# One decoder layer on one core: attention values summed by query tile, split, mean and exponential moved, first and last stage rearranged

## The chip, the core and the metric

The kernel runs on one core of a Trainium2 chip. TensorE (PE) multiplies, VectorE (DVE), ScalarE (ACT) and GpSimd (POOL) work on tiles in SBUF, SyncE (SP) issues most DMAs. The metric is the device time of one execution in microseconds (us); smaller is better. The inputs lie in HBM, and the output goes back there.

## The reference

One layer over 256 tokens of width 2048, in float32. A normed input is projected; 16 query heads in 4 groups attend in three branches (compressed blocks, selected blocks, window), a convolution module works beside them, both go through one output projection, and a gated feed-forward block follows.

```python
h = rms_norm(x, mix_norm_g[l])
proj = h @ w_in[l]
q, kv, gate_logits, conv_in = jnp.split(proj, splits, axis=-1)
...
attn = nsa_attention(q, kv, gates, rel_bias, cmp_pos[l], cmp_w1[l], cmp_w2[l])
conv = conformer_conv(conv_in, conv_w[l], conv_b[l], conv_ln_g[l], conv_ln_b[l])
x = x + jnp.concatenate([attn, conv], axis=-1) @ w_out[l]
h = rms_norm(x, ffn_norm_g[l])
x = x + conv_glu_ffn(h, w_up[l], ffn_conv_w[l], ffn_conv_b[l], w_down[l])
```

At 256 tokens there are only four selectable blocks, so "selected" and "window" both are causal attention over all keys, each with its own keys and values; each query tile therefore has, per head, two softmaxes of 256 queries by up to 256 keys, and one over 15 compressed keys. The convolution module gates, convolves 31 taps per channel, subtracts the mean over channels, divides by the deviation and applies a swish.

## The kernel before

**Numbers in two halves.** Each float32 operand is split into a high part in the fast matmul format (made by ACT, a cast) and a low part (the rest, by DVE or POOL, a subtraction). A product is three matmuls: high by high, high by low, low by high (`mm3`, L142 to L144; `mm_rows`, L149 to L151). Weights come in chunks of 1 MB, one DMA each on SP's queue (L91), three buffers deep, and are split two chunks ahead (`w_split`: ACT L110; DVE or, for chunks 5 to 31, POOL at L115).

**Stages.** (1) A head: the first two weight chunks (chunk 0 and 1, the gate and value halves of convolution channels 0 to 127) come packed with the transposed input in six pieces (`CUTS`: four pieces of 2 of the 16 blocks of the inner dimension, then two pieces of 4); each piece is split by ACT (L234, L239) and DVE (L235, L240) and multiplied at once into banks 0 and 1. (2) The other convolution inputs, keys and values, with the convolution's taps on DVE beside them. (3) Eight query chunks (`tile_chunk`), each 128 columns, and the attention of their heads. (4) The output projection, the feed-forward up and down products. (5) The last rows: sums of squares, a power on POOL (L174), scaling on ACT (L1019) and DVE (L1020), output DMAs (L1022).

**What sets the order around the change.** The order is written by hand: each engine executes in the order of the program. A chunk of 48 matmuls has four hooks, one after each 12. A hook may run an attention tick (`attn_tick`), the steps that queue behind (`behind`, `conf`, `steps`), and one piece of a weight split. `late` holds what is done when the next chunk begins, such as taking a finished query tile out of its bank (`q_out`: DVE L638).

**Attention.** A query tile i has four units n = 4i .. 4i+3: two head halves r times two branches br. A tick with number n does the values of unit n-7 (`st_out`, L770, L774), the transposes of unit n-5 (L754), the scores of a pair of units when n is even (`st_scores`, L712, L713; bank 2 and bank 4 or 5), the reciprocal of sums (`st_rec`, L741, L742), the bias and minimum (`st_min`, DVE L722, reads the scores), the copy of transposes (`st_evac`, ACT L759), the scaling (`st_scale`, POOL L748) and the exponential (`st_exp`, ACT L733). The values of both r are summed when the second r of a branch is there: once for br 0, and once for br 1, the latter followed by the compressed values (L774) and the split of the result (L776, L777).

**Beside it.** The compressed branch of a tile pair m runs in steps: scores (L657), logits and exponential (`cmp_exp`, L663 to L672), probabilities (L677 to L680), transposes (L685). The convolution's mean (`conf_mean`, L430, and its copy L426), the subtraction from y (`conf_apply`, DVE L444, 128x512), squares (ACT L449) and their sums (DVE L452) are steps of `conf`, started by `conf_center` when query chunk 1 begins. The query's split (`q_split`) makes a high part on ACT (L644) and a low part on DVE (L645), at a hook.

```python
for f, d in ((st_out, DEEP), (st_transpose, D_T), (st_scores, 0), (st_rec, D_S), (st_min, 1),
             (st_evac, D_T), (st_scale, D_S), (st_exp, 1)):
```

Of the kernel before, what the change touches and what calls it, by code (L numbers as in the profile page):

```python
# [17 lines left out]
P = 128  # L18
# [21 lines left out]

def head_of_slot(s):
    i, r = divmod(s, 2)
    return (i // 4) * 8 + r * 4 + i % 4
# [3 lines left out]
def hybrid_trunk(ctx: ExitStack, tc: tile.TileContext, a: dict, out: bass.AP):  # L47
# [31 lines left out]
    st = {"dma": 2, "split": 2, "use": 0}  # L79
# [110 lines left out]
    with ExitStack() as mx:  # L190
# [27 lines left out]
        for _ in range(3):  # L218
            w_dma()
# [11 lines left out]
        for (lo, hi), (xc, *wc) in zip(CUTS, heads):  # L231
            for k in range(lo, hi):
                xk = xc[:, (k - lo) * T:(k - lo + 1) * T]
                nc.scalar.activation(xt_h[:, k], xk, AF.Copy, scale=mix_g[:, k:k + 1])  # L234
                nc.vector.scalar_tensor_tensor(xt_l[:, k], xk, mix_g[:, k:k + 1], xt_h[:, k].bitcast(F32),  # L235
                                               op0=OP.mult, op1=OP.subtract)
            sl = slice(lo * P, hi * P)
            for (h, l), raw in zip((parts[0], parts[1]), wc):
                nc.scalar.activation(h[:, sl], raw, AF.Copy)  # L239
                nc.vector.tensor_sub(l[:, sl], raw, h[:, sl].bitcast(F32))  # L240
# [107 lines left out]
        ysum = wk.tile([P, T], F32, name="ysum", bufs=1)  # L348
        summed = []

        def conf_add(j):
            summed.append(j)
            if len(summed) > 1:
                nc.vector.tensor_add(ysum, y[:, summed[0]] if len(summed) == 2 else ysum, y[:, j])
# [37 lines left out]
        for j in range(8):  # L392
            gb, ab = [b[:, :T] for b in bank[2 * (j if j < 3 else (j + 1) % 2):][:2]]
            if j == 0:
                pair = [w_next(2), w_next(2, 1)]
                for lo, hi in CUTS:
                    for ps, (wh, wl) in zip((gb, ab), pair):
                        for k in range(lo, hi):
                            sl = slice(k * P, (k + 1) * P)
                            mm3(ps, wh[:, sl], wl[:, sl], xt_h[:, k], xt_l[:, k], k == 0, k == KD - 1)  # L400
                w_pump()
                first = gb, ab
                continue
            tile_chunk(gb)
# [17 lines left out]
        cf = {}  # L422

# [56 lines left out]
        def conf_center():  # L480
            conf.extend((
                no, no, conf_mean, no, lambda: conf_apply(OP.subtract, 0), lambda: conf_apply(OP.subtract, 2),
                lambda: conf_sq(0, 0), lambda: (conf_sq(2, 2), conf_apply(OP.subtract, 4)),
                lambda: conf_apply(OP.subtract, 6), lambda: conf_fold(2, 2),
                lambda: conf_sq(4, 2), no, lambda: conf_fold(2, 2), lambda: conf_sq(6, 2), no,
                lambda: conf_fold(2, 2), no, lambda: conf_fold(1, 1)))
# [153 lines left out]

        def q_split(i):
            for r in range(2):
                h, o = slice(64 * r, 64 * r + 64), slice(64 - 64 * r, 128 - 64 * r)
                nc.scalar.activation(qs[h, i % 4, r], q32[i][h], AF.Copy)  # L644
# [4 lines left out]
        pct = ap.tile([P, 4, T], F32, name="pct", tag="oh")  # L649
        pcb = ap.tile([P, 2, 4, 32], F32, name="pcb")  # L650
        nc.gpsimd.memset(pcb[:, :, :, NCMP:], 0.0)

# [8 lines left out]
        def cmp_exp(m):  # L661
            cm["e"] = e = wk.tile([P, 2, 4, NCMP], F32, name="ec", bufs=1)
            nc.gpsimd.memset(e[:, 0, :, NC0:], BIG)  # L663
# [5 lines left out]
            mn = wk.tile([P, 2, 4], F32, name="mnc", bufs=1)  # L669
            nc.vector.tensor_reduce(mn, e, axis=mybir.AxisListType.X, op=OP.min)  # L670
            nc.vector.tensor_sub(e, e, mn[:, :, :, None].to_broadcast([P, 2, 4, NCMP]))
            nc.scalar.activation(e, e, AF.Exp, scale=-1.0)  # L672
# [9 lines left out]
        def cmp_tr(m):  # L682
# [4 lines left out]
            nc.scalar.activation(pct[:, m], pg[:, :T], AF.Copy)  # L687
# [69 lines left out]
        def st_evac(n):  # L757
            es = wk.tile([P, 384], F32, name="es", bufs=5)
# [3 lines left out]
        def st_out(n):  # L762
            i, r, br = units[n]
            if r == 0:
                return
            es, o, q = [US.pop(n - 2), US.pop(n)], bank[7], i // 4
            kw = dict(skip_group_check=True)
            for b, cols in enumerate((slice(0, T), slice(P, T))):
                for rr in range(2):
                    nc.tensor.matmul(o[64 * rr:64 * rr + 64, cols], vt[:, b, br, q, rr],  # L770
                                     es[rr][:, :T] if b == 0 else es[rr][:, T:], start=br + b == 0, stop=False, **kw)
            if br == 1:
                assert cbst["done"] > i // 2
                nc.tensor.matmul(o[:, :T], vc[:, i % 2, i // 4].rearrange("p r n -> p (r n)"), pct[:, i // 2],  # L774
                                 start=False, stop=True, **kw)
                nc.scalar.activation(ma_h[:, i], bank[7][:, :T], AF.Copy)  # L776
# [359 lines left out]
```

## Time and profile before

| what | us |
| --- | --- |
| median of 3 runs | 1116.58 |
| lowest, highest | 1116.53, 1116.62 |
| profiled execution, its own time | 1115.1 |
| its span, first to last instruction | 1113.3 |
| PE busy in the span | 1098.0 |
| DVE, ACT, POOL busy | 770.4, 577.6, 188.1 |

The page counts an engine as busy while an instruction runs on it; times within the span are measured from its start. A wait is idle time of an engine before an instruction, put down to what came last. Matmul ends are modelled, so idle time of PE between two matmuls reads a little short; distances from start to start are exact. The granted TensorE clock is 0.998 over the span.

### The profile page before, as it was taken

Reading aid. Unit: us, or ns where it says so; the run is one execution under the profiler, and the core shown is the slowest. Engines: PE = TensorE matmul, PEld = TensorE weight load, DVE = VectorE, ACT = ScalarE, POOL = GpSimd, SP = SyncE. Lnnn points to the kernel's source line nnn. Section 1 sums busy time; section 2 is a strip of 40 time slices with the busy share of each in tenths; the row PEclk is TensorE's granted clock in tenths of the full one; section 3 lists DMA queues with packets and bytes.
Section 4 is the critical chain, followed back from the end, with each engine's and each line's share of the span. In section 5 each row is a group of like instructions: output and inputs, shape, how many; then the busy total and the mean of one; then the engine's idle time right before and its main releaser. Section 6 shows DMA issues by size and latency. Waiting matters only on the chain.

```text
span 1113.3 us, 16297 instructions
## 1 busy us (share of the span) xinstructions
PE 1098.0 (99%) x6506; PEld 956.6 (86%) x6506; DVE 770.4 (69%) x1262; ACT 577.6 (52%) x836; POOL 188.1 (17%) x143
## 2 busy tenths in 40 slices
PE   9999999899999999999999999999999999999997
PEld 8999999887788888888888888888888888888885
DVE  6799976766456677777777777777778655556554
ACT  7544456777465555554555455545555444444442
POOL 0888765665200000000000000000000000000000
PEclk9999999999999999999999999999999999999999
DMA  9685537222644655555555555555555555555542
GB/s 373 221 295 199 172 98 258 77 81 97 233 171 173 232 190 192 189 190 190 189 189 189 190 189 189 189 190 189 189 189 190 189 188 189 189 189 187 188 155 76
DMA packets 32425, 207.46 MB, mean 186 GB/s; under 512 B 3883, under 2 KB 6203, under 8 KB 8284
## 3 DMA queue, kind: packets, MB, share of 16 engines
q1 hardware_dynamic: 28972, 199.85, 50.4%
q10 hardware_dynamic: 3376, 6.55, 1.6%
q8 instruction: 51, 0.84, 0.3%
q14 instruction: 26, 0.21, 0.0%
HBM read 204.27 MB, written 2.12 MB: 185 GB/s over the span
## 4 chain that ended last, share of the span: by engine, by line
PE 93%; DVE 2%; ACT 1%; POOL 1%; DMA 1%; issue 1%; SPq 0%; POOLq 0%; DVEq 0%; ACTq 0%
PE bank L972 29%; PE bank L990 21%; PE bank L974 14%; PE bank L142 5%; PE bank L144 5%; PE bank L143 5%; PE bank L149 3%; PE bank L150 3%; PE bank L151 3%; PE bank L770 1%; POOL e L748 1%; DMA hb<-in_head 1%; PE bank L754 1%; ACT e L733 0%; PE bank L518 0%
## 5 line engine op out<-in xcount | busy, mean ns | idle before, releaser
L110 ACT ACTIVATE wh<-wraw 128x2048 fp32r<-128x2048 f32 (+2 forms) x239 | 355.7, 1505 | 361.5 <-issue 150.7
L115 DVE TENSOR_TENSOR wl<-wraw,wh 128x2048 fp32r<-128x2048 f32 (+1 forms) x185 | 364.9, 1977 | 195.4 <-ACT wh L110 195.3
L972 PE MATMUL bank<-xt,wh 128*128 128x512 f32 x1408 | 488.7, 394 | 0.0
L974 PE MATMUL bank<-xt,wl 128*128 128x256 f32 x1408 | 390.1, 277 | 0.0
L972 PEld LDWEIGHTS bank<-xt,wh 128*128 128x128 f32 x1408 | 264.0, 188 | 61.2
L974 PEld LDWEIGHTS bank<-xt,wl 128*128 128x128 f32 x1408 | 264.4, 188 | 0.0
L142 PE MATMUL bank<-xt,wh 128*128 128x256 f32 x512 | 146.7, 287 | 1.4 <-ACT wh L239 1.4
L144 PE MATMUL bank<-xt,wl 128*128 128x256 f32 x512 | 145.0, 283 | 0.3 <-DVE wl L240 0.2
L143 PE MATMUL bank<-xt,wh 128*128 128x256 f32 x512 | 144.8, 283 | 0.0
L174 POOL TENSOR_TENSOR rstd<-ms,half 128x1 f32<-128x1 f32 x4 | 2.2, 548 | 809.2 <-DVE ms L167 809.2
L115 POOL TENSOR_TENSOR wl<-wraw,wh 128x1024 fp32r<-128x1024 f32 (+1 forms) x54 | 121.4, 2275 | 28.0 <-ACT wh L110 26.9
L990 PE MATMUL bank<-wh,gh 128*128 128x512 f32 x336 | 105.5, 395 | 0.0
L990 PE MATMUL bank<-wl,gh 128*128 128x512 f32 x336 | 105.5, 395 | 0.0
L990 PE MATMUL bank<-wh,gl 128*128 128x512 f32 x336 | 105.5, 395 | 0.0
L142 PEld LDWEIGHTS bank<-xt,wh 128*128 128x128 f32 x512 | 98.0, 191 | 3.2 <-ACT wh L239 1.9
L144 PEld LDWEIGHTS bank<-xt,wl 128*128 128x128 f32 x512 | 98.0, 191 | 0.7 <-DVE wl L240 0.7
L143 PEld LDWEIGHTS bank<-xt,wh 128*128 128x128 f32 x512 | 98.0, 191 | 0.4
L369 DVE SCALAR_TENSOR_TENSOR bank<-us,cw,bank 128x256 f32<-128x256 f32 x232 | 94.9, 482 | 2.8 <-ACT bank L364 2.1
L935 DVE SCALAR_TENSOR_TENSOR yt<-u,fcw,yt 128x255 f32<-128x255 f32 (+1 forms) x176 | 80.9, 481 | 3.1
L990 PEld LDWEIGHTS bank<-wl,gh 128*128 128x128 f32 x336 | 63.0, 187 | 15.5
L990 PEld LDWEIGHTS bank<-wh,gl 128*128 128x128 f32 x336 | 63.0, 187 | 15.4
L990 PEld LDWEIGHTS bank<-wh,gh 128*128 128x128 f32 x336 | 62.9, 187 | 15.4
(188 smaller groups left out, 1073.8 us busy)
## 6 DMA issues: line engine op xcount, KB each, us to landing
wraw<-in_w_u SPq DMA_DIRECT2D x88, 1024.0 KB, 4.8
wraw<-in_w_d SPq DMA_DIRECT2D x44, 1024.0 KB, 4.8
wraw<-in_w_t SPq DMA_DIRECT2D x30, 1024.0 KB, 5.0
wraw<-in_w_o SPq DMA_DIRECT2D x16, 1024.0 KB, 4.8
wraw<-in_w_vg SPq DMA_DIRECT2D x4, 608.0 KB, 3.7
hb<-in_head SPq DMA_DIRECT2D x2, 1024.0 KB, 9.7
xr<-in_x SPq DMA_DIRECT2D x2, 1024.0 KB, 19.8
wb<-rel_scratch ACTq DMA_DIRECT2D x1, 2048.0 KB, 14.3
```

What stands on the lines that cost most here:

```text
L110: nc.scalar.activation(h[:, sl], raw[:, sl], AF.Copy)
L115: (nc.gpsimd if pooled else nc.vector).tensor_sub(l[:, sl], raw[:, sl], h[:, sl].bitcast(F32))
L142: nc.tensor.matmul(ps, wh, xh, start=first, stop=False)
L143: nc.tensor.matmul(ps, wh, xl, start=False, stop=False)
L144: nc.tensor.matmul(ps, wl, xh, start=False, stop=last)
L149: nc.tensor.matmul(ps, xh, wh, start=first, stop=False)
L150: nc.tensor.matmul(ps, xh, wl, start=False, stop=False)
L369: nc.vector.scalar_tensor_tensor(y[:, j] if last else acc[0], us[:, j, k:k + T], cw[:, j, k:k + 1], acc[0], op0=OP.mult, op1=OP.add)
L935: nc.vector.scalar_tensor_tensor(ys[i][:, d:], us_[i][:, :T - d], fcw[:, c, k:k + 1], ys[i][:, d:], op0=OP.mult, op1=OP.add)
L972: nc.tensor.matmul(bk[i], wh[:, k, sl], xt[:, kt].rearrange("p a t -> p (a t)"), start=kt == 0, stop=False)
L974: nc.tensor.matmul(bk[i][:, :T], wl[:, k, sl], xt_h[:, kt], start=False, stop=kt == KD - 1)
L990: nc.tensor.matmul(banks[n], g[p][:, kt % 4, sl], ws[w][:, k * 1024 + n * 512:k * 1024 + (n + 1) * 512], start=kt + i == 0, stop=i == 2 an ...
```

## The change

The numbers of operations hardly change; places do.

- **Head.** The weights of the third chunk (chunk 2, the gate half of channels 128 to 255) are loaded in two halves, the first between pieces 4 and 5 of the head, the second after piece 6, and multiplied in the head (`next_mm`: blocks 0 to 7 after piece 4, blocks 8 to 15 after piece 6). The first piece's weights are cast by DVE, and its matmuls run all high products of both banks first (`first_mm`).
- **Convolution's mean** starts when query chunk 0 begins, in bank 1; subtractions and squares are packed closer. Its sum and the compressed probabilities share one buffer.
- **Exponential's table** is loaded by a two-element exponential behind the gates.
- **Query split:** the high part follows at once on taking the tile out (`q_high`).
- **Compressed logits** go to a tile of their own, whose masked part is filled once; probabilities come one step sooner for the first three pairs.
- **Attention tick:** the minimum stands ahead of the reciprocal; the values of all four units of a tile run as one group, with one more buffer for the copies.
- **Last rows:** the last sum of squares runs on DVE with the mean in it; the result leaves in pieces of 256, 256 and 512 columns, the very last on ACT's queue.

```diff
+HEAD_NEXT = (0, 0, 0, 8, 8, 16)
...
+            if n == 3:
+                raw2 = wpool.tile([P, CW], F32, name="wraw", bufs=NR)
+            if n in (3, 5):
+                sl = slice((n - 3) * 512, (n - 1) * 512)
+                nc.sync.dma_start(raw2[:, sl], a["w_t"][0][:, sl])
-        for _ in range(3):
+        for _ in range(2):
             w_dma()
...
+            if part == 1:
+                nc.vector.tensor_sub(l[:, sl], raw, h[:, sl].bitcast(F32))
+            elif n == 0:
+                nc.vector.tensor_copy(h[:, sl], raw)
+            else:
                 nc.scalar.activation(h[:, sl], raw, AF.Copy)
...
+                for n, hi in enumerate(HEAD_NEXT):
+                    head_mm((gb, ab), n) if n else first_mm((gb, ab))
+                    w = parts[2] if n < len(CUTS) - 1 else w_next(2, 2)
+                    w_pump()
+                    next_mm(g1, w, at, hi)
+                    at = hi
...
-            cf["b"] = bank[0][:, :T]
-            nc.tensor.matmul(cf["b"], ones, ysum, start=True, stop=True)
+            cf["b"] = bank[1][:, :T]
+            nc.tensor.matmul(cf["b"], ones, cf["sum"], start=True, stop=True)
...
+            ready = wk.tile([P, 2], F32, name="rv", bufs=1)
+            nc.scalar.activation(ready, ones[:, :2], AF.Exp)
...
+        def q_high(i):
+            for r in range(2):
+                h = slice(64 * r, 64 * r + 64)
+                nc.scalar.activation(qs[h, i % 4, r], q32[i][h], AF.Copy)
...
-                nc.scalar.activation(qs[h, i % 4, r], q32[i][h], AF.Copy)
...
+        ecr = ap.tile([P, 2, 4, NCMP], F32, name="ecr")
+        nc.gpsimd.memset(ecr, BIG)
...
-            nc.gpsimd.memset(e[:, 0, :, NC0:], BIG)
...
-                       ((lambda m: None, cmp_scores, cmp_exp, lambda m: None, cmp_probs, lambda m: None, cmp_tr) if m < 3 else
+                       ((lambda m: None, cmp_scores, cmp_exp, cmp_probs, lambda m: None, cmp_tr) if m < 3 else
...
-            i, r, br = units[n]
-            if r == 0:
+            i = n // 4
+            if n % 4 < 3:
                 return
...
+            for br in range(2):
+                es = [US.pop(4 * i + 2 * r + br) for r in range(2)]
...
-            for f, d in ((st_out, DEEP), (st_transpose, D_T), (st_scores, 0), (st_rec, D_S), (st_min, 1),
+            for f, d in ((st_out, DEEP), (st_transpose, D_T), (st_scores, 0), (st_min, 1), (st_rec, D_S),
...
             q_evac(i, bank[i % 2])
+            q_high(i)
             behind.append(lambda: q_split(i))
...
-            if i == 1:
+            if i == 0:
                 fill(1e9)
                 conf_center()
...
+                    nc.vector.tensor_tensor_reduce(out=sqd3, in0=xq, in1=xq, scale=1.0 / D, scalar=acc, op0=OP.mult,
+                                                   op1=OP.add, accum_out=ss3[:, t, 4:5])
...
+            for lo, hi in ((0, 256), (256, 512), (512, 1024)):
...
+                (nc.scalar if lo == 512 and t else nc.sync).dma_start(
```

Three places as the built programs have them. First, DVE where the reciprocal, the compressed probabilities (smc, pcb) and the convolution's subtraction (y) stand between the third query tile's split (qs) and the minimum of unit 6 (e, mn from bank 66, which is bank 2, first half), before the change:

```order
L645 TENSOR_TENSOR qs<-q_2519,qs 64x256 x2
L444 TENSOR_TENSOR y<-y,ck 128x512
L677 TENSOR_REDUCE smc<-ec 128x8
L678 RECIPROCAL smc<-smc 128x8
L679 TENSOR_TENSOR smc<-smc,gates 128x8
L680 TENSOR_TENSOR pcb<-ec,smc 128x8x15
L741 RECIPROCAL lsum<-lsum 128x4
L742 TENSOR_TENSOR lsum<-lsum,gates 128x4
L722 ISA e,mn<-bank_66,wb 128x128
```

And DVE at the same place after it (the lines are those of the changed program: L702 takes the tile out, L713 is the split, L794 the minimum, L813 and L814 the reciprocal):

```order
L747 TENSOR_REDUCE smc<-ec 128x8
L748 RECIPROCAL smc<-smc 128x8
L749 TENSOR_TENSOR smc<-smc,gates 128x8
L750 TENSOR_TENSOR pcb<-ec,smc 128x8x15
L702 SCALAR_TENSOR_TENSOR q_2532<-bank_64,rB 128x256
L794 ISA e,mn<-bank_66,wb 128x128
L794 ISA mn 128x1
L794 ISA e,mn<-bank_68,wb 128x256
L794 ISA mn 128x1
L713 TENSOR_TENSOR qs<-q_2532,qs 64x256 x2
L794 ISA e,mn<-bank_66,wb 128x128
```

The subtraction is gone from there, the probabilities stand ahead of the tile that is taken out, and between the split and the minimum of unit 6 nothing stands. Second, PE where the values of query tile 0 are summed into bank 71 (bank 7), before: the first of its two groups (br 0), and what followed it; the second group (br 1) came after 12 matmuls in all:

```order
L770 MATMUL bank_71<-es,vt 64x256 x2
L770 MATMUL bank_71<-es,vt 64x128 x2
L754 MATMUL bank_67<-ident,e 128x128 x3
L142 MATMUL bank_65<-xt,wh 128x256
L143 MATMUL bank_65<-xt,wh 128x256
L144 MATMUL bank_65<-xt,wl 128x256
```

PE at the values of the same tile after the change:

```order
L147 MATMUL bank_64<-xt,wl 128x256
L845 MATMUL bank_71<-es,vt 64x256 x2
L845 MATMUL bank_71<-es,vt 64x128 x2
L845 MATMUL bank_71<-es,vt 64x256 x2
L845 MATMUL bank_71<-es,vt 64x128 x2
L847 MATMUL bank_71<-pct,vc 128x256
L826 MATMUL bank_70<-ident,e 128x128 x3
```

Both branches now stand side by side, at the tick where the second one stood. Third, ACT from the last gates to the first split query tile, before the change:

```order
L624 ACTIVATE gates<-bank_67,rc 128x16 x3
L110 ACTIVATE wh<-wraw 128x1024 x2
L644 ACTIVATE qs<-q_2314 64x256 x2
L110 ACTIVATE wh<-wraw 128x1024 x2
L426 ACTIVATE ck<-bank_64 128x256
L733 ACT_TABLE_LOAD
L733 ACTIVATE e,lsum<-e,mn 128x128
```

And ACT from the same gates after it:

```order
L686 ACTIVATE gates<-bank_67,rc 128x16 x3
L689 ACT_TABLE_LOAD
L689 ACTIVATE rv<-ones 128x2
L113 ACTIVATE wh<-wraw 128x1024 x2
L488 ACTIVATE ck<-bank_65 128x256
L511 ACTIVATE s_2315<-y 128x512
L708 ACTIVATE qs<-q_2325 64x256 x2
```

The table's load, the mean's copy (ck) and the first squares now stand ahead of the first split query tile.

More of the change, by code (lines that the diff above doesn't have):

```diff
@@ L78, in hybrid_trunk @@
     NR, NB, LA = 3, 3, 2
-    st = {"dma": 2, "split": 2, "use": 0}
+    st = {"dma": 3, "split": 3, "use": 0}
     raws, parts, pieces = {}, {}, []
@@ L230, in hybrid_trunk, with head_x @@
             parts[c] = (wpool.tile([P, CW], F32R, name="wh", bufs=NB), wpool.tile([P, CW], F32R, name="wl", bufs=NB))
-        for (lo, hi), (xc, *wc) in zip(CUTS, heads):
-            for k in range(lo, hi):
-                xk = xc[:, (k - lo) * T:(k - lo + 1) * T]
+        def head_x(n, k, part):
+            lo = CUTS[n][0]
+            xk = heads[n][0][:, (k - lo) * T:(k - lo + 1) * T]
+            if part == 0:
                 nc.scalar.activation(xt_h[:, k], xk, AF.Copy, scale=mix_g[:, k:k + 1])
+            else:
@@ new lines, in head_split, with head_mm @@
+        def head_split(n):
+            ks = range(*CUTS[n])
+            if n == 0:
+                for c in range(2):
+                    head_w(n, c, 0)
+            for k in ks:
+                head_x(n, k, 0)
+                head_x(n, k, 1)
+            for c in range(2):
+                if n:
+                    head_w(n, c, 0)
+                head_w(n, c, 1)
+        def head_mm(pss, n):
+            for ps, (wh, wl) in zip(pss, (parts[0], parts[1])):
+                for k in range(*CUTS[n]):
+                    sl = slice(k * P, (k + 1) * P)
+                    mm3(ps, wh[:, sl], wl[:, sl], xt_h[:, k], xt_l[:, k], k == 0, k == KD - 1)
@@ new lines, in first_mm, with next_mm @@
+        def first_mm(pss):
+            for part in range(3):
+                for k in range(*CUTS[0]):
+                    sl = slice(k * P, (k + 1) * P)
+                    for ps, w in zip(pss, (parts[0], parts[1])):
+                        nc.tensor.matmul(ps, w[part == 2][:, sl], (xt_h, xt_l)[part == 1][:, k],
+                                         start=k + part == 0, stop=False)
+        def next_mm(ps, w, lo, hi):
+            wh, wl = w
+            for k in range(lo, hi):
+                sl = slice(k * P, (k + 1) * P)
+                mm3(ps, wh[:, sl], wl[:, sl], xt_h[:, k], xt_l[:, k], k == 0, k == KD - 1)
@@ L394, in hybrid_trunk @@
             if j == 0:
[L395 to L401, printed above, removed]
+                g1 = bank[2][:, :T]
+                parts[2] = h2, l2 = [wpool.tile([P, CW], F32R, name=nm, bufs=NB) for nm in ("wh", "wl")]
+                for n in range(len(CUTS)):
+                    head_split(n)
+                    if n in (3, 5):
+                        sl = slice((n - 3) * 512, (n - 1) * 512)
+                        nc.scalar.activation(h2[:, sl], raw2[:, sl], AF.Copy)
+                        nc.vector.tensor_sub(l2[:, sl], raw2[:, sl], h2[:, sl].bitcast(F32))
+                w_dma()
+                st["use"] = 2
+                at = 0
+                for n, hi in enumerate(HEAD_NEXT):
[4 more added lines that the diff above has]
+                    at = hi
+                parts.pop(0), parts.pop(1)
                 first = gb, ab
                 continue
-            tile_chunk(gb)
+            if j > 1:
+                tile_chunk(gb)
             if j == 1:
@@ L686, in cmp_tr @@
                                  is_transpose=True, start=True, stop=True)
-            nc.scalar.activation(pct[:, m], pg[:, :T], AF.Copy)
+            if m == 0:
+                cm["t"] = ap.tile([P, 4, T], F32, name="pct", tag="oh")
+            nc.scalar.activation(cm["t"][:, m], pg[:, :T], AF.Copy)
             cbst["done"] = m + 1
@@ L762, in st_out @@
         def st_out(n):
-            i, r, br = units[n]
-            if r == 0:
+            i = n // 4
+            if n % 4 < 3:
                 return
-            es, o, q = [US.pop(n - 2), US.pop(n)], bank[7], i // 4
+            o, q, m = bank[7], i // 4, i // 2
+            assert cbst["done"] > m
             kw = dict(skip_group_check=True)
[L768 to L776, printed above, removed]
-                nc.vector.tensor_sub(ma_l[:, i], bank[7][:, :T], ma_h[:, i].bitcast(F32))
+            for br in range(2):
+                es = [US.pop(4 * i + 2 * r + br) for r in range(2)]
+                for b, cols in enumerate((slice(0, T), slice(P, T))):
+                    for r in range(2):
+                        nc.tensor.matmul(o[64 * r:64 * r + 64, cols], vt[:, b, br, q, r],
+                                         es[r][:, :T] if b == 0 else es[r][:, T:], start=br + b == 0, stop=False, **kw)
+            nc.tensor.matmul(o[:, :T], vc[:, i % 2, q].rearrange("p r n -> p (r n)"), cm["t"][:, m],
+                             start=False, stop=True, **kw)
+            nc.scalar.activation(ma_h[:, i], o[:, :T], AF.Copy)
+            nc.vector.tensor_sub(ma_l[:, i], o[:, :T], ma_h[:, i].bitcast(F32))
         tick = {"n": 0}
```

59 lines of the change are left out of this document (32 added, 27 removed).

## The prediction

> **What bounds the kernel now.** I read the page's busy times first, then the busy times by stage, then what PE waited for, then the timeline around those waits.
>
> ```profile
> PE 1098.0 (99%) x6506; PEld 956.6 (86%) x6506; DVE 770.4 (69%) x1262; ACT 577.6 (52%) x836; POOL 188.1 (17%) x143
> ...
> 0.00:20.00 20.00, 17.28 (x118) 16.37 (x119) 14.15 (x32) 15.59 (x33) 0.69 (x6) 1.00 0.92 361
> 200.00:280.00 80.00, 75.88 (x561) 64.20 (x561) 54.78 (x215) 61.15 (x182) 51.40 (x59) 1.00 0.26 93
> 1104.00:1114.00 10.00, 1.08 (x10) 0.88 (x8) 2.81 (x9) 2.73 (x8) 0.55 (x1) 0.71 0.53 197
> ```
>
> PE is busy for 1098.0 of 1113.3 us, so only three stages can give anything: the head, where it idles 2.7 of 20 us, the attention, where it idles 4.1 of 80, and the end, where 8.9 of 10 pass without it. Outside them only less work or a cheaper order on PE helps. Clock is full (1.00) wherever PE works.
>
> ```profile
> PE bank L712 <- DVE mn L722: 3.7, 4, 2.1
> PE bank L142 <- ACT wh L239: 1.4, 2, 1.1
> ```
>
> PE's waits have names: scores wait for DVE's minimum (four times, the longest 2.1 us), and the head waits for a cast. After the attention PE never idles long again, and its later work doesn't depend on when it starts (weights are there: 0.2 us idle from 280 to 1104), so what is won before 280 reaches the end whole.
>
> **The attention's waits.** This is DVE ahead of the two longest, in rows of its timeline, and PE at the longest:
>
> ```profile
> 199.99 0.28 DVE L670 TENSOR_REDUCE mnc<-ec 128x8 f32<-128x120 f32 x1 [1.20 <-POOL ec L663]
> 200.79 0.28 DVE L722 CUSTOM_DVE_ANT_0 e<-bank,wb 128x128 f32<-128x128 f32 x1
> ...
> 205.07 0.86 DVE L645 TENSOR_TENSOR qs<-q,qs 64x256 fp32r<-64x256 f32 x2 [1.02 <-ACT qs L644]
> 205.94 0.69 DVE L444 TENSOR_TENSOR y<-y,ck 128x512 f32<-128x512 f32 x1
> 206.55 0.27 DVE L677 TENSOR_REDUCE smc<-ec 128x8 f32<-128x120 f32 x1
> 207.49 0.17 DVE L741 RECIPROCAL lsum<-lsum 128x4 f32<-128x4 f32 x1
> 207.78 0.28 DVE L722 CUSTOM_DVE_ANT_0 e<-bank,wb 128x128 f32<-128x128 f32 x1
> 207.99 0.42 DVE L722 CUSTOM_DVE_ANT_0 e<-bank,wb 128x256 f32<-128x256 f32 x1
> ...
> 205.64 0.49 PE L754 MATMUL bank<-ident,e 128*128 128x128 f32 x3
> 208.22 0.36 PE L712 MATMUL bank<-k_h,qs 128*128 128x256 f32 x1 [2.09 <-DVE mn L722]
> ```
>
> Scores of a new pair overwrite bank 2, whose last reader is the first part of the minimum, so PE at 208.22 waits for the minimum of 207.78. Ahead of it stand 1.02 us in which DVE waits for ACT's cast of the query, 0.69 for the convolution's subtraction, 0.94 for the compressed probabilities (206.55 to 207.49) and 0.29 for the reciprocal (207.49 to 207.78). The change takes the first away (the cast follows the tile at once), moves the second a chunk earlier and the third ahead of the tile, and puts the fourth behind. It removes 2.9 us from a place where PE lost 2.1. The wait before 201 had one cause: DVE stood 1.20 us for POOL, which filled the masked part of the logits behind its scalings; the tile filled once ends that. The other two waits of this kind are the 205 one over again, without the subtraction.
>
> PE's idle time in 200 to 280 is 4.1 us by the row above. From start to start it is more: three transposes end PE's part at 205.97 if each takes the 0.11 that separates their starts, so 205.97 to 208.22 is 2.25, where the page says 2.09; six waits of this stage (the four, and one each for POOL's scaling and the logits) are 0.16 longer than shown, 5.1 us in all.
>
> What is late next: I laid the new order out by hand with these durations. PE reaches the query chunks 1.1 us earlier (below). DVE now does four subtractions (2.8 us) and two weight parts before the first two tiles are split; by my layout the first scores find their query ready within 0.1 us. The minimum of unit 6 ends its first part just as PE comes to the scores, where it came 2.3 late. Closest behind are POOL's scalings:
>
> ```profile
> 201.04 4.31 POOL L748 TENSOR_SCALAR e<-e,lsum 128x128 f32<-128x128 f32 x4 [1.08 <-ACT ec L672]
> 203.93 0.44 PE L754 MATMUL bank<-ident,e 128*128 128x128 f32 x2 [0.22 <-POOL e L748]
> ```
>
> Four scalings took 4.31 us, two ticks' worth, and PE already waited 0.22 for them. Without the other waits, ticks come faster, and the reciprocal starts them a minimum (0.7 us) later in its tick. I leave 1.0 us of waits for the first ten ticks. Removed: 5.1 - 1.0 = **4.1 us**; bounds 1.5 (half of it comes back through POOL or DVE) and 5.1.
>
> [...]
>
> **The values in one group.**
>
> ```profile
> 210.51 0.28 PE L144 MATMUL bank<-xt,wl 128*128 128x256 f32 x1
> 210.72 0.87 PE L770 MATMUL bank<-es,vt 128*64 128x256 f32 x8
> 211.52 0.55 PE L754 MATMUL bank<-ident,e 128*128 128x128 f32 x3
> 211.83 0.37 PE L142 MATMUL bank<-xt,wh 128*128 128x256 f32 x1
> ...
> 210.99 0.39 PE L770 MATMUL bank<-es,vt 128*64 128x256 f32 x2
> 211.21 0.39 PE L770 MATMUL bank<-es,vt 128*64 128x128 f32 x4
> ...
> 228.84 0.28 PE L144 MATMUL bank<-xt,wl 128*128 128x256 f32 x1
> 228.96 0.49 PE L754 MATMUL bank<-ident,e 128*128 128x128 f32 x3
> 229.21 0.36 PE L142 MATMUL bank<-xt,wh 128*128 128x256 f32 x1
> ```
>
> A tick with one group takes 1.32 us from its last L144 to the next L142 (210.51 to 211.83), one without 0.37 (228.84 to 229.21): a group by itself costs 0.95. It has four pairs; inside it a 256-wide pair takes 0.22 (210.99 to 211.21), and the rest of 0.95 is entering and leaving. Placed behind another group, it needs at most its own 0.80 (210.72 to 211.52) and at least what its pairs stream: 0.22 twice, and for the 128-wide pairs half of that, 0.66. So each of eight tiles saves 0.15 to 0.29; nearest is the low end of cost, since no change of shape is left between the groups: 0.26 x 8 = **2.1 us**. Bounds 0 (the last copy, made two ticks before, comes late and PE waits for it) and 2.3.
>
> **The table.**
>
> ```profile
> 189.45 1.28 ACT L733 ACT_TABLE_LOAD   x1
> 190.75 0.40 ACT L733 ACTIVATE e<-e,mn 128x128 f32<-128x128 f32 x1
> ```
>
> The load takes 1.28 us, and the next operation starts 0.02 after. It moves to about 180, ahead of the mean's copy, for which PE now waits before it may write bank 1 in query chunk 1. In my layout the copy ends 0.7 us before that. So it costs nothing, and its gain is inside the waits above. If cover were gone, PE would wait at that chunk's start, once. [...]
>
> **The head.**
>
> ```profile
> 11.21 1.71 ACT L234 ACTIVATE xt<-hb,ha 128x256 fp32r<-128x256 f32 x4 [0.68 <-DMA hb<-in_head]
> 13.49 0.39 PE L142 MATMUL bank<-xt,wh 128*128 128x256 f32 x1 [1.05 <-ACT wh L239]
> 13.99 1.71 ACT L234 ACTIVATE xt<-hb,ha 128x256 fp32r<-128x256 f32 x4
> 17.73 4.78 DVE L115 TENSOR_TENSOR wl<-wraw,wh 128x1024 fp32r<-128x1024 f32 x4 [0.17 <-ACT wh L110]
> ...
> 31.88 0.54 DVE L261 TENSOR_SCALAR xdg<-ident,rc 128x128 f32<-128x128 f32 x1 [0.23 <-POOL rc L257]
> 33.52 0.60 PE L266 MATMUL bank<-xdg,ones 128*128 128x128 f32 x4
> ```
>
> PE waits 1.05 us for the fifth piece, whose DMA landed at 11.21. The two large pieces start 2.78 us apart (11.21, 13.99), so the half chunk put in front (0.5 MB) delays the fifth by 1.39, to 12.6. Against the wait and that delay, together 2.4, stand 24 more matmuls, 0.12 each by the starts above, 2.9 us. They need the half's low part: DVE subtracts 1024 columns in 1.2 us (a quarter of 4.78), by my layout from 11.5 to 12.7, and PE gets there at 12.5. So the wait closes but for 0.2. The casts that go to DVE let the first high products start up to 0.4 earlier; DVE's extra two (such a cast is not shown; between 0.28, the smallest wide DVE row above, and 0.54, L261) delay the low parts by as much again and cancel most of it. That would be 1.3 to 1.6 us. But the matmuls L266, at 33.52, need the diagonal that DVE finishes at 32.42, behind input DMAs that the change doesn't make earlier: PE can come 1.1 earlier there and no more. Gain **1.1 us**; bounds 0 and 1.3. From 33 to 178 the order of DVE's taps shifts by one or two, and PE has no wait there now, so I count 0.
>
> **The end.**
>
> ```profile
> 1105.12 0.42 DVE L1014 TENSOR_TENSOR x<-bank,x 128x256 f32<-128x256 f32 x1 [0.34 <-PE bank L151]
> 1106.47 0.55 POOL L174 TENSOR_TENSOR rstd<-ms,half 128x1 f32<-128x1 f32 x1 [4.96 <-DVE ms L167]
> 1107.06 1.41 DVE L1020 SCALAR_TENSOR_TENSOR x<-x,rstd,gfin 128x512 f32<-128x512 f32 x2 [0.66 <-POOL rstd L174]
> 1107.88 1.20 SPq L1022 DMA_DIRECT2D out<-x  x2
> ```
>
> From the last addition to the power pass 1.35 us, through ACT and back. After it DVE does add, one 256-wide operation with accumulation (0.42 by L722) and its read, 1.1 in all with one more small operation ahead: 0.2 saved. Scaling takes three operations for two, 1.4 us as before; the last DMA is as large, and starts from a free queue instead of behind another issue: 0.1. Sum **0.3**; bounds -0.3 (more, smaller packets) and 0.7.
>
> **Sum.** 4.1 + 2.1 + 1.1 + 0.3 = 7.6 us against the profiled execution's own 1115.1, so 1107.5. The median shown, 1116.6, lies 1.5 above that execution; the same 7.6 off it gives **1109.0**.
>
> **Rivals.**
>
> *POOL or DVE takes the minimum's place* (chance 0.18). For: PE's 0.22 us wait for POOL, and 51.4 busy us in 80. Against: POOL idles the rest. Half the waits return: 1116.6 - 7.6 + 2.6 = 1111.6.
>
> *Grouping saves nothing* (0.10), because the copies come late or the shapes don't matter: 1109.0 + 2.1 = 1111.1.
>
> *The change doesn't do what it says* (0.06): the head's half chunk delays the next pieces as much as it covers, and the attention's waits only move; what is left is the grouping or less: 1114.5 to 1116.5.
>
> *Slower, by ACT* (0.05). ACT executes in order, and the high part now stands right behind the tile that DVE takes out, ahead of copies and weight casts. It is busy 61.2 of 80 us in the attention, and the change shortens that stage by about 6, so it has 13 us left, for six tiles about 2.1 each. Where DVE brings the tile later than that, ACT paces the stage; from 3.7 us late per tile, it costs 9.8 us, which ends 2.2 slower than now, at 1118.8. Against: by my layout the third tile, the worst, is 1.9 late.
>
> **Chances and range.** Forecast 0.61, within 1107.3 to 1110.5. To hold 8 in 10 the range must take in the first two rivals and both bounds of the head and the end: all terms at their best give 9.4, 1107.2; the first two rivals alone give 1111.6, both together 1113.7, which is a small part of their chance. I say 1107.0 to 1112.8. About 0.2%, 2.2 us, is what a measurement of this kernel can tell from no change. Faster than that 0.89, within it 0.06, slower 0.05.
>
> **What would show it.** In the changed profile: waits of scores on DVE's minimum under 0.6 us in total (now 3.7); no wait of DVE on POOL's fill or on ACT's query cast; records of values in runs of 16; 200 to 274 holding what 200 to 280 holds now; no PE wait above 0.5 us in the head; the last DMA issue 0.3 closer to the last matmul. Wrong would be: long rows of PE waiting for POOL's scaling, for ACT's copies, or for the mean's copy.

## The result, and the profile after

The changed kernel takes 1108.78 us (median of four runs, 1107.50 to 1109.34) where the kernel before takes 1116.55 beside it: a ratio of 0.9932, 95% interval 0.9915 to 0.9949. The profiled execution took 1109.11 us, its span is 1107.3: 6.0 us less than the profiled execution before, though the medians lie 7.8 apart. Executions of the kernel before come in two groups, 15 of 35 at 1114.9 to 1115.3 and 17 at 1116.5 to 1116.8 (the other three at 1117.1 to 1118.2), and the profile shows one of the first group.

These are the page's busy times of the changed kernel:

```profile
PE 1095.6 (99%) x6506; PEld 960.7 (87%) x6506; DVE 772.4 (70%) x1268; ACT 575.6 (52%) x833; POOL 186.4 (17%) x140
```

And its busy times by stage (stretch, its length, then PE, PEld, DVE, ACT, POOL with counts, clock, DMA share, GB/s):

```profile
0.00:20.00 20.00, 18.54 (x127) 17.46 (x128) 14.24 (x34) 14.04 (x30) 0.69 (x6) 1.00 0.90 350
200.00:274.00 74.00, 72.71 (x556) 64.36 (x555) 51.92 (x205) 58.19 (x178) 48.88 (x57) 1.00 0.28 100
1098.00:1108.00 10.00, 1.43 (x13) 1.22 (x11) 3.59 (x11) 2.58 (x7) 0.55 (x1) 0.80 0.54 192
```

PE idles 1.5 us in the first 20 (2.7 before), and 1.3 in the attention (4.1 before). What it still waits for, again as line, releaser, total, times, longest, without a wait of 1.0 us ahead of the first matmul, which both kernels have, and two of 0.2:

```profile
PE bank L826 <- POOL e L820: 1.2, 1, 1.2
PE bank L145 <- DVE sg L433: 0.9, 1, 0.9
```

No score waits for DVE's minimum any more, and no cast is waited for in the head. The first row is new in size: transposes wait for POOL's scaling. The second is new altogether, and stands where the prediction counted nothing. This is PE in the timeline there, at the first key/value chunk:

```profile
100.86 0.28 PE L147 MATMUL bank<-xt,wl 128*128 128x256 f32 x1
101.99 0.36 PE L145 MATMUL bank<-xt,wh 128*128 128x256 f32 x1 [0.85 <-DVE sg L433]
```

That chunk writes the bank that DVE reads for the gate of the last convolution chunk. To see why DVE is late, go back along DVE's timeline to the last operation that is longer than before. It is the negation of the bias table's slots, 32x16 numbers:

```profile
62.03 0.48 DVE L421 SCALAR_TENSOR_TENSOR bank<-us,cw,bank 128x256 f32<-128x256 f32 x1
62.57 0.07 DVE L332 MEMSET rbn<- 1x16 f32 x1
62.67 4.55 DVE L333 TENSOR_SCALAR rbn<-rbn 32x16 f32<-32x16 f32 x1
67.14 1.25 DVE L421 SCALAR_TENSOR_TENSOR bank<-us,cw,bank 128x256 f32<-128x256 f32 x3
```

It took 4.55 us; in the kernel before, the same operation took 0.27:

```profile
57.37 0.27 DVE L283 TENSOR_SCALAR rbn<-rbn 32x16 f32<-32x16 f32 x1
```

POOL's timeline says what it stood for. These are POOL's last two weight subtractions of a run of ten:

```profile
62.44 4.75 POOL L118 TENSOR_TENSOR wl<-wraw,wh 128x1024 fp32r<-128x1024 f32 x2
```

They end at 67.19, the negation at 67.22. In the kernel before it ended at 57.64, also 0.03 behind the end of a POOL subtraction, but it had begun only 0.24 ahead of that end. The taps, which have an operand in PSUM, run beside POOL at their usual 0.48. The change hadn't touched the negation: it is a step that the chunks call one by one, and since the head now takes the first of these chunks in, it slid from the 93rd to the 108th place among DVE's operations. From the starts of the same matmuls in both timelines, PE is 1.09 us ahead of the profile before at 18.75, 0.87 at 95.22, 0.14 **behind** at 101.99, 5.57 ahead after the attention (287.13), 5.65 at the last matmul.

### The profile page after: what moved, and what is told of

It is laid out like the page before. It is cut to its first block, busy times and chain, and to the rows that moved or that the text cites. A ratio compares the mean times of both kernels' runs of the same rounds, so it can differ in the third digit from the quotient of the medians.

```text
span 1107.3 us, 16289 instructions
## 1 busy us (share of the span) xinstructions
PE 1095.6 (99%) x6506; PEld 960.7 (87%) x6506; DVE 772.4 (70%) x1268; ACT 575.6 (52%) x833; POOL 186.4 (17%) x140
## 4 chain that ended last, share of the span: by engine, by line
PE 88%; DVE 7%; DMA 2%; ACT 1%; issue 1%; POOL 0%; SPq 0%; POOLq 0%; DVEq 0%; ACTq 0%
PE bank L1046 29%; PE bank L1064 21%; PE bank L1048 15%; DVE bank L421 4%; PE bank L145 3%; PE bank L147 3%; PE bank L146 3%; PE bank L152 3%; PE bank L153 3%; PE bank L154 3%; PE bank L845 1%; DMA hb<-in_head 1%; DMA wraw<-in_w_t 1%; PE bank L826 1%; DVE wl L118 1%
## 5 line engine op out<-in xcount | busy, mean ns | idle before, releaser
L118 DVE TENSOR_TENSOR wl<-wraw,wh 128x2048 fp32r<-128x2048 f32 (+1 forms) x183 | 360.9, 1977 | 195.9 <-ACT wh L113 194.4
```

The costliest lines, as they stand in the source:

```text
L118: (nc.gpsimd if pooled else nc.vector).tensor_sub(l[:, sl], raw[:, sl], h[:, sl].bitcast(F32))
```

## The experiments

Theories at the start: **the shared port**, as the expectations call it (DVE's small operation, and POOL's scaling at 207, both with all operands in SBUF, each stood still while the other engine's operation ran; a port itself no run shows, only these waits and where they end), against **the order of the taps** (DVE is simply full from 60 to 100). The intervals in the table are wide, because the kernel before has two groups, and they overlap; so variants are compared by the ranges of their executions, and time lost or won is read from the profiles. Runs e1 to e4 were made on one chip, e5, e6, e7 and e11 on a second, e9 and e12 to e14 on a third, so a difference of 0.3 us between medians says little.

| run | median us | range | ratio to before, 95% |
|---|---|---|---|
| changed kernel | 1108.78 | 1107.50 to 1109.34 | 0.9932 (0.9915 to 0.9949) |
| negation on ACT (e1) | 1107.93 | 1107.60 to 1108.08 | 0.9923 (0.9911 to 0.9936) |
| values in two groups (e2) | 1108.85 | 1108.81 to 1110.12 | 0.9935 (0.9923 to 0.9948) |
| old head (e3) | 1108.91 | 1108.77 to 1109.33 | 0.9933 (0.9919 to 0.9946) |
| one scaling on DVE (e4) | 1107.06 | 1106.97 to 1108.47 | 0.9920 (0.9908 to 0.9933) |
| e1 and e4 together (e5) | 1107.02 | 1106.86 to 1107.32 | 0.9919 (0.9904 to 0.9934) |
| e1, reciprocal first (e6) | 1107.65 | 1106.99 to 1108.25 | 0.9924 (0.9910 to 0.9939) |
| e1, query cast late (e7) | 1109.12 | 1108.83 to 1109.32 | 0.9937 (0.9920 to 0.9953) |
| e1, old table load (e9) | 1108.13 | 1107.82 to 1108.20 | 0.9927 (0.9912 to 0.9942) |
| e1, fill each time (e11) | 1109.01 | 1108.81 to 1109.05 | 0.9936 (0.9922 to 0.9951) |
| five negations on DVE (e12) | 1109.63 | one run | |
| before, negation on ACT (e13) | 1116.54 | 1115.03 to 1116.84 | 1.0000 (0.9991 to 1.0009) |
| before again (e14) | 1115.12 | one run | |

**The negation on ACT (e1).**

```diff
-            nc.vector.tensor_scalar_mul(rbn[:32], rbn[:32], -1.0)
+            nc.scalar.activation(rbn[:32], rbn[:32], AF.Copy, scale=-1.0)
```

> The changed kernel, with the negation of the bias table's slots (32x16) on ACT instead of DVE. Theory, the shared port: the 4.55 us that DVE spent on it at 62.67 were a wait for POOL's run of subtractions, so DVE gains about 4.3 us there, the gate's product on which the first key/value chunk waits ends well before PE comes, the 0.9 us wait at 101 goes, the query chunks start 1.3 us earlier, and the span falls by 1.0 to 1.5 us: about 1107.5 us median. Rival, the order of the taps: DVE is full from 60 to 100 whatever the negation costs, the wait at 101 stays above 0.5 us, and the time stays at 1108.8.

ACT needs 0.20 us for it, and PE's timeline has the key/value chunk following at once:

```profile
100.86 0.28 PE L147 MATMUL bank<-xt,wl 128*128 128x256 f32 x1
100.98 0.28 PE L145 MATMUL bank<-xt,wh 128*128 128x256 f32 x1
```

The wait is gone, the span falls by 1.2 to 1106.1, and the median by 0.9. The ranges overlap: one of the changed kernel's four executions, 1107.50, is as fast as e1's, as it would be if its negation had a shorter wait; it has no trace. The taps' order falls. That the operation stood for POOL, and isn't slow by itself, the next run shows.

**Five negations on DVE (e12).**

```diff
-        steps.extend([lambda: None] * 19 + [tab_neg] + ...
+        steps.extend([lambda: None] * 7 + [probe, lambda: None, lambda: None] * 4 + [tab_neg] + ...
+        def probe():
+            nc.vector.tensor_scalar_mul(rbn[:32], rbn[:32], -1.0)
```

> The changed kernel with the negation of the bias table done five times on DVE (an odd number, so the table is the same), at five places of POOL's run of ten subtractions instead of one. A probe of the length, not of the time. Theory, the shared port: each takes as long as it has to stand until a POOL subtraction ends (0.1 to 2.4 us), and now and then one more of them (up to 4.8); each ends within 0.05 us behind the end of one. Rival, the operation is slow by itself or by what lies ahead of it on DVE: all five take the same, or their ends stand in no relation to POOL's.

The five in DVE's timeline, and POOL's run in its own, two subtractions to a row:

```profile
47.15 1.18 DVE L336 TENSOR_SCALAR rbn<-rbn 32x16 f32<-32x16 f32 x1
52.17 0.90 DVE L336 TENSOR_SCALAR rbn<-rbn 32x16 f32<-32x16 f32 x1
56.85 0.95 DVE L336 TENSOR_SCALAR rbn<-rbn 32x16 f32<-32x16 f32 x1
62.10 0.45 DVE L336 TENSOR_SCALAR rbn<-rbn 32x16 f32<-32x16 f32 x1
65.83 1.44 DVE L333 TENSOR_SCALAR rbn<-rbn 32x16 f32<-32x16 f32 x1
...
43.52 4.78 POOL L118 TENSOR_TENSOR wl<-wraw,wh 128x1024 fp32r<-128x1024 f32 x2 [1.10 <-ACT wh L113]
48.26 4.78 POOL L118 TENSOR_TENSOR wl<-wraw,wh 128x1024 fp32r<-128x1024 f32 x2
52.99 4.78 POOL L118 TENSOR_TENSOR wl<-wraw,wh 128x1024 fp32r<-128x1024 f32 x2
57.74 4.79 POOL L118 TENSOR_TENSOR wl<-wraw,wh 128x1024 fp32r<-128x1024 f32 x2
62.50 4.75 POOL L118 TENSOR_TENSOR wl<-wraw,wh 128x1024 fp32r<-128x1024 f32 x2
```

Add start and length: the negations end at 48.33, 53.07, 57.80, 62.55 and 67.27, the pairs of POOL at 48.30, 53.04, 57.77, 62.53 and 67.25. Each length is the time that was left to the end of a subtraction. All five took the first chance, as did those in the profiles of e2 (2.17 us) and e4 (2.18), where PE didn't wait at 101; the profiled execution of the changed kernel missed one chance and stood for a second subtraction. The five take 4.92 us together, and in this profile PE waits 1.0 us for the same gate again.

The convolution's running sum (`ysum`, 128x256, both inputs in SBUF) does the same with a longer operation: alone it takes 0.42 us (at 102.11 in the kernel before), and at 94.46 there it took 2.20 and ended 0.28 behind the end of a POOL subtraction. Not every DVE operation in SBUF stands: a comparison of one column (128x1, at 173.18 in the kernel before) took 0.15 us while a POOL subtraction ran from 173.06 to 175.52.

In e12, then, the negation's wait lasts to the end of a POOL subtraction, with 0.02 to 0.03 us between end and end. Why DVE stands, and why the comparison didn't, no run shows. That a waiting operation can be passed over once rests on the one case of 4.55 us.

**The old head (e3).** The head of before in the changed kernel (the half chunk in front, its 24 matmuls in the head and the casts on DVE taken out):

```diff
-    st = {"dma": 3, "split": 3, "use": 0}
+    st = {"dma": 2, "split": 2, "use": 0}
...
-            if j > 1:
-                tile_chunk(gb)
+            tile_chunk(gb)
```

> The changed kernel with the head of before (no half chunk in front, all casts on ACT), the rest as changed. Here the negation stands again 16 places earlier in DVE's order. Theory, the gain of the head was given back at the wait for DVE at 101: the first key/value chunk starts at 101.8 as in the kernel before and 0.1 earlier than in the changed one, so the time is that of the changed kernel within 0.3 us, 1108.6. Rival, the head's gain reaches the end: 0.9 to 1.1 us slower, 1109.8.

PE runs 0.9 to 1.1 us later than in the changed kernel up to 96, and starts the key/value chunk at

```profile
101.87 0.28 PE L145 MATMUL bank<-xt,wh 128*128 128x256 f32 x1
```

0.12 earlier. Its negation takes 0.26 us. The head's whole gain was given back at 101 in the profiled execution; the medians (1108.91 against 1108.78) agree. Against e1, where PE doesn't wait at 101 either, the head is worth 0.98 in the median and 0.89 at that matmul.

**One scaling on DVE (e4).** In the changed kernel PE's other wait has three rows, one each of POOL, DVE and PE:

```profile
206.14 2.84 POOL L820 TENSOR_SCALAR e<-e,lsum 128x128 f32<-128x128 f32 x2 [1.29 <-DVE lsum L814]
...
207.04 1.23 DVE L118 TENSOR_TENSOR wl<-wraw,wh 128x1024 fp32r<-128x1024 f32 x1
...
209.03 0.44 PE L826 MATMUL bank<-ident,e 128*128 128x128 f32 x2 [1.20 <-POOL e L820]
...
216.77 1.50 POOL L820 TENSOR_SCALAR e<-e,lsum 128x128 f32<-128x128 f32 x2 [1.90 <-ACT es L831]
```

The pair of scalings for unit 4 takes 2.84 us where an undisturbed pair, in the last row, takes 1.50: 1.34 more, 0.31 of it beside a fold of DVE (an addition of squares, 205.88 to 206.57) and 1.04 beside its weight part. By the recorded starts POOL's second scaling came first here, 207.02 against 207.04, and yet it is the one that stood, so the recorded starts don't tell which of two engines gets its way.

```diff
-                nc.gpsimd.tensor_scalar_mul(e[:, lo:hi], e[:, lo:hi], lsum[:, br, t:t + 1])
+                (nc.vector if n in (4,) else nc.gpsimd).tensor_scalar_mul(e[:, lo:hi], e[:, lo:hi],
+                                                                         lsum[:, br, t:t + 1])
```

> The changed kernel, with the scaling of unit 4 alone (two of 64 operations) on DVE instead of POOL. Theory, the shared port: at 207.02 POOL's second operation of this unit stands behind DVE's weight subtraction (1.96 us in place of 0.92) and PE waits 1.36 from start to start for it; on DVE it costs 0.3 to 0.7 us and nothing waits. The wait of transposes for POOL goes from 1.2 to under 0.2, no other wait above 0.5 takes its place, time 1107.6. Rival: PE then waits for scores or for the next unit's scaling instead, because DVE and POOL are both behind by that much here: 1108.5 to 1109.3.

In DVE's timeline, and PE's, of this run:

```profile
204.76 0.67 DVE L820 TENSOR_SCALAR e<-e,lsum 128x128 f32<-128x128 f32 x2
...
207.79 0.39 PE L145 MATMUL bank<-xt,wh 128*128 128x256 f32 x1 [0.26 <-ACT pct L759]
```

The wait for POOL is gone and 0.26 for a copy of ACT has come. The attention is 0.9 shorter (below). The remaining gain over the changed kernel's profile, 1.24 at the start of the attention, is the negation that here took its first chance.

**Values in two groups (e2).**

```diff
-            i = n // 4
-            if n % 4 < 3:
+            i, r, br = units[n]
+            if r == 0:
                 return
-            for br in range(2):
-                es = [US.pop(4 * i + 2 * r + br) for r in range(2)]
+            es, o, q = [US.pop(n - 2), US.pop(n)], bank[7], i // 4
```

> The changed kernel, with the values of a query tile again in two groups, each two ticks after its copies. Theory of the prediction: one group saves 0.26 us for each of 8 tiles, so this run is 2.1 us slower than the changed kernel, 1110.9. Rival, grouping saves nothing: 1108.8. A third possibility: the two groups shift PE against POOL and the 1.2 us wait for POOL's scaling changes by itself; then the values' own rows (start of the group to the next operation) decide, not the total.

By the total, grouping is worth nothing against the changed kernel, but the totals compare different executions: here the negation took its first chance. The stage itself is compared from the fourth query chunk to a matmul of the output projection that is the same in both, with e4; each of the two has a single wait of 0.2 to 0.3 us there. PE's timeline of e2, then of e4:

```profile
198.37 0.28 PE L145 MATMUL bank<-xt,wh 128*128 128x256 f32 x1
...
286.90 0.40 PE L152 MATMUL bank<-wh,ma_h 128*128 128x512 f32 x1
```

```profile
198.50 0.28 PE L145 MATMUL bank<-xt,wh 128*128 128x256 f32 x1
...
284.98 0.39 PE L152 MATMUL bank<-wh,ma_h 128*128 128x512 f32 x1
```

88.53 against 86.48: one group saves 2.05 us. The changed kernel needs 87.39, so of these 2.05 it keeps 1.14. These are its two rows, behind those of the kernel before, which needs 93.36:

```profile
199.34 0.28 PE L142 MATMUL bank<-xt,wh 128*128 128x256 f32 x1
...
292.70 0.40 PE L149 MATMUL bank<-wh,ma_h 128*128 128x512 f32 x1
```

```profile
199.74 0.28 PE L145 MATMUL bank<-xt,wh 128*128 128x256 f32 x1
...
287.13 0.39 PE L152 MATMUL bank<-wh,ma_h 128*128 128x512 f32 x1
```

The length of this stage repeats well from profile to profile: 87.40 and 87.41 in e1 and e12, 86.47 in e5, 93.36 in e14; only e3, whose recorded clock is 0.947, has 87.88 with the same attention. The reason for the lost part is in e2's waits: its longest for POOL is 0.2 us, though POOL's pair for unit 4 takes 2.85 us there too. There the first group of values, some 0.95 us of PE's work, stands ahead of the transposes of unit 4 and covers POOL's delay. Grouping takes that cover away.

**Both remedies (e5).** The edits of e1 and e4.

> The changed kernel with both remedies: the negation on ACT and the scaling of unit 4 on DVE. Theory, two separate costs of the shared port: no wait at 101 in any execution and none for POOL at 207, so the best time of the run with the scaling moved (1107.0) in every execution: median 1106.8, all within 0.8 us. Rival, the spread has another cause: times still spread over 1.5 us, median 1107.1 or more.

No wait at 101 and none for POOL; 1106.86 to 1107.32, a spread of 0.46 us, and all four below the changed kernel's lowest. The median is 0.2 above what was expected and not to be told from e4's. None of the four goes over 1107.4, where one of e4's five reached 1108.47; with so few executions this hints that e1 adds steadiness, and no more.

**The attention's parts, undone one at a time on e1.** The reciprocal ahead of the minimum:

```diff
-(st_min, 1), (st_rec, D_S),
+(st_rec, D_S), (st_min, 1),
```

> The changed kernel with the negation on ACT (1107.9 so far), and the reciprocal again ahead of the minimum in a tick. Theory: DVE stands at the reciprocal until ACT has the exponentials (1.43 us of DVE idle at 210.26 in the changed kernel), the minimum behind it comes late and scores wait for it again, 0.5 to 2 us in all; POOL's scaling starts no earlier where the exponential is what comes last, so its 1.2 us wait stays: 1108.4 to 1110. Rival, the order of these two is worth nothing now that the other causes are gone: 1107.9 within 0.3.

In its waits of PE, one has gone down and one has come back:

```profile
PE bank L784 <- DVE mn L794: 0.8, 1, 0.8
PE bank L826 <- POOL e L820: 0.6, 1, 0.6
```

Together 1.4, where e1 has 1.2 for POOL; the stage of the attention takes 87.40 in both, and the median is 0.3 lower, inside the uncertainty. My theory was wrong: this order is worth nothing here.

The query's high part cast late, just ahead of the subtraction:

```diff
-            q_high(i)
             behind.append(lambda: q_split(i))
...
+                nc.scalar.activation(qs[h, i % 4, r], q32[i][h], AF.Copy)
                 nc.vector.tensor_sub(qs[o, i % 4, r], q32[i][h],
```

> The changed kernel with the negation on ACT (1107.9), and the query's high part again cast behind the chunk's next piece, just ahead of the subtraction that needs it. Theory of the prediction: DVE waits about 1.0 us for ACT's cast at each of eight tiles, in the first three of them scores wait for the minimum behind it, 0.5 to 1.0 us each: 1109 to 1110.5. Rival: the slack that the other parts of the change made holds this too: 1107.9 within 0.3.

DVE's waits have the cast again, eight times:

```profile
DVE qs L714 <- ACT qs L713: 7.6, 8, 1.0
```

1.2 us slower than e1, as expected; but scores don't wait for the minimum. PE waits for POOL twice, 1.8 us in all, where e1 has the second of these waits alone, 1.2: the 1.0 us that DVE stands reach the transposes through the reciprocal and POOL's scalings, and 0.85 of the loss is at the first of the two (198.62). Another 0.4 comes at 261.56; its cause stays open.

The fill before every use:

```diff
             e = ecr
+            nc.gpsimd.memset(e[:, 0, :, NC0:], BIG)
```

> The changed kernel with the negation on ACT (1107.9), and POOL again filling the masked part of the compressed logits before every use. Theory of the prediction: the fill queues behind POOL's scalings, DVE waits about 1 us for it in the first pair of tiles, and scores wait 0.5 to 1.0 us once; later pairs have slack: 1108.4 to 1109. Rival: 1107.9 within 0.3, the wait before 201 had another cause beside the fill.

DVE's timeline has the wait back, [1.12 <-POOL] at 198.88, and 1.1 us are lost against e1: 0.4 where scores come late (199.83), and 0.6 where transposes wait for POOL (202.88), a wait that e1 doesn't have.

The table's load back at the first exponential (the two lines of `ready` left out):

> The changed kernel with the negation on ACT (1107.9), and the exponential's table again loaded at the first exponential instead of behind the gates. Prediction: the move is worth nothing by itself, 1107.9 within 0.3. Rival: the load delays the first exponentials by 1.3 us, the reciprocals and POOL's scalings with them, and transposes wait for POOL by 0.5 to 1.3 us more: 1108.4 to 1109.2.

0.2 slower, inside the uncertainty: next to nothing, as predicted. The profile has a wait of 0.2 for POOL at 202.18 that e1 has not: the rival's mechanism, but under its 0.5 to 1.3.

**The two groups of the kernel before (e13, e14).** The edit of e1 on the kernel before; and that kernel profiled once more.

> The kernel before with one edit, the negation on ACT. Its executions fall in two groups, near 1115.0 and near 1116.6, and its profile is of the first. Theory: in the second group DVE's negation misses its turn at the port and waits for one or two POOL subtractions more, 2.4 to 4.8 us, which the 2.5 us of slack at the first key/value chunk doesn't hold; without it all executions are near 1115.0. Rival, the two groups have another cause (the sums of the convolution on DVE, which also wait for POOL, or the transfers): the median stays at 1116.6 and both groups remain.

> The kernel before, unchanged, for a second profile of it. Theory: if this execution is of the group near 1116.6, DVE's negation at about 57 is longer than the 0.27 us of the first profile by a whole POOL subtraction or two and PE waits for DVE at 101.8; if it is near 1115.0, it looks as the first did. Rival: an execution near 1116.6 whose negation takes 0.3 us and which loses its 1.5 us at another place.

Both groups stay (5 executions near 1115.1, 6 near 1116.7), so the negation is not their cause. The second profile of before fell in the first group again and looks as the first did. But the profile of e13 fell in the second group, at a span of 1115.0, and shows it. Up to 208 its PE is as in the kernel before, with the same wait of 2.1 us. Then the busy times of one stretch, of e13 and of the kernel before:

```profile
209.00:212.00 3.00, 3.00 (x16) 2.78 (x14) 2.35 (x11) 3.00 (x10) 3.00 (x3) 0.54 0.00 0
```

```profile
209.00:212.00 3.00, 3.00 (x27) 2.55 (x26) 2.35 (x11) 3.00 (x10) 3.00 (x3) 1.00 0.00 0
```

In 3 us PE does 16 matmuls instead of 27, at a granted clock of 0.54. In its timeline 256-wide matmuls follow each other in 0.21 us instead of 0.12:

```profile
208.33 0.36 PE L712 MATMUL bank<-k_h,qs 128*128 128x256 f32 x1 [2.08 <-DVE mn L722]
...
210.05 0.41 PE L142 MATMUL bank<-xt,wh 128*128 128x256 f32 x1
210.26 0.41 PE L143 MATMUL bank<-xt,wh 128*128 128x256 f32 x1
```

1.5 us are lost there, and no idle time shows it. The other executions have no trace, only a mean clock: spans of 1113.1 to 1113.5 go with 0.997 or 0.998, longer ones with 0.995 to 0.997, most with 0.996. Three microseconds at half clock would lower the mean by 0.0013 (an estimate, 1.5 us in 1113), so it fits; that each of the longer ones has this drop is not shown. In e13 the drop comes right behind 2.1 us of idling, with 0.7 and 0.2 in the 8 us ahead: the granted clock is 1.00 from 208.2 to 209, and 0.61, 0.50, 0.50 and 0.68 in the four microseconds from there. That the idling is the cause is argued from this one trace. Both profiles of the kernel before have the same wait; the first keeps a clock of 1.00 behind it, and the second has the span, 1113.3, and the mean clock, 0.998, of the first. What makes one execution lose the clock there and another not, no run shows.

## Why the prediction was right, and where only by luck

1109.0 was predicted and 1108.78 measured, but the sum of 7.6 us meets the profiles at 6.0, and two errors of opposite sign make up for it.

- **Attention's waits, predicted 4.1, and grouping, 2.1.** Together 5.97 measured (93.36 us before from 199.34 to 292.70, 87.39 after). Six waits of 5.1 were cut to one of 1.36, so 3.7, where 1.0 had been left for POOL; grouping by itself is worth 2.05. The two are not independent: without grouping (e2) the stage is 4.8 shorter than before, and grouping took away the cover of POOL's delay. The causes named were right in part: cast and fill are worth 1.2 and 1.1 undone singly, the reciprocal's place nothing; and undone, the cast makes transposes wait rather than scores. That the subtractions' and the probabilities' new places bring the rest was not tried.
- **POOL, rival one.** It did take the minimum's place once, beside one fold and one weight part of DVE: by 1.34 us, where the rival has half the waits return, 2.6. The prediction's own row of four scalings, 4.31 us, shows the like when taken apart: the second took 2.25 us, starting at 201.62 beside a weight part and a subtraction of DVE, against 0.92 for the fourth, of the same shape, at 204.43.
- **The head, 1.1.** 1.09 up to the diagonal, 0.87 after it: the cap held, and was tighter than thought, since DVE finished the diagonal at 32.71 instead of 32.42.
- **"From 33 to 178 ... I count 0."** This step failed, by 1.0 to 1.3 us in the profiled execution. I saw that the taps shift by places, and asked only whether PE waits there now. The slack at the key/value chunk was 2.5 us (DVE's gate ended at 99.34 and PE came at 101.85); the head used 0.9 of it, and a small operation of DVE that lands on another spot beside POOL's run cost 4.28 more, nearly two of POOL's subtractions. That PE lost no more is luck as well: the two running sums ahead of the gate happened to stand less, 1.70 us instead of 3.56, and the gate ended only 2.5 later.
- **From span to median.** I took the sum off a median of the second group, with rows from an execution of the first. The change removes the 2.1 us wait and, if e13's trace stands for that group, the drop of the clock behind it: 1.5 us that no term of the sum has. Against 1115.1 the measured gain is 6.3, and 7.2 with the negation out of the way.
- **The end, 0.3.** From the last matmul's start to the span's end 8.15 instead of 8.50.
- **The table, 0.** e9 finds 0.2, inside the uncertainty.
- **A slip.** In the rival on ACT, six tiles 3.7 late each against 13 us left give 9.2 and not 9.8; nothing hangs on it.

Added up, 0.87 for the head, 1.27 lost from there to the fourth query chunk, 5.97 for the attention, 0.1 behind it and 0.35 for the end are the 6.0 of the spans.

## What to carry to other kernels

Where DVE and POOL both work on operands in SBUF, read each one's long rows against the other's ends: an operation whose length follows the other engine's finish is waiting, although the profile calls it busy (five of five in e12, 0.02 to 0.03 us from end to end). When work moves by some places, ask of every DVE operation that reads and writes only SBUF what POOL does at its new place, above all of tiny ones that nobody prices. And before a sum is taken off a median, see whether the profiled execution and the median are of one kind: behind a PE wait of 2.1 us, one traced execution (e13) also had a granted clock of 0.54 over three microseconds.

## What the runs showed of the hardware that was not expected

- A 32x16 operation of DVE took 0.26 to 4.55 us, by where in POOL's run of 2.4 us subtractions it fell; on ACT 0.20.
- Behind 2.1 us of PE idling the granted clock was at about a half for some 3 us in e13 (0.54), and at 1.00 in the kernel before, whose profile has the same wait.
- The profile of e3 records a clock of 0.947, while the 256-wide matmuls of its chunks start 0.12 us apart (101.75, 101.87, 101.99) as in e1 (100.86, 100.98). Its attention is 0.48 us longer than e1's, 87.88 against 87.40, and the execution took 1109.33 us, the changed kernel's 1109.11. So a recorded clock 5% lower did not make the kernel 5% slower.
